# Zero-padded queries, reordered SSM output taps, an idle-tile first chunk and one merged gate/up stream in a decoder kernel

## The chip, the cores and the metric

The kernel runs on one core of a Trainium2 chip. The metric is the device time of one execution in microseconds (us). The engines are TensorE (PE in the profile, its weight loads apart as PEld), VectorE (DVE), ScalarE (ACT), GpSimd (POOL) and SyncE (SP), which here only issues DMAs.

## The reference

A batch of one, 256 positions, width 1024. Four decoder layers, each a mixer and a SwiGLU feed-forward block (FFN, hidden width 2816), and then a second block with attention and a state-space model (SSM) side by side:

```
for i in range(4):                                     # first_block
    hn = rms_norm(x, g[i, 0])
    m = (diff_attention, stick_breaking_attention, sliding_window_sink_attention)[i % 3](hn, ...)
    x = x + rms_norm(m, g[i, 1])
    h = rms_norm(x, g[i, 2])
    x = x + rms_norm((silu(h @ w_gate) * (h @ w_up)) @ w_down, g[i, 3])
# second_block
q, k, v, gate_a, u, gate_s = split(rms_norm_2(x, mix_norm) @ w_in)
attn = dilated_mixture_attention(q, k, v, ...) * silu(gate_a)       # 8 heads of 64
ssm  = s5_glu(u, ...) * silu(gate_s)                                # 32 groups of 16 channels, 64 complex states
x = x + concat(attn, ssm) @ w_out
x = x + sigmoid(rms_norm_2(x, ple_norm) @ w_ple_gate) * (p @ w_ple_proj)
```

Every head has 64 dimensions (the values of the differential attention 128). In the SSM the states follow x_t = a x_(t-1) + (B u)_t with complex a, and y = Re(C x) + D u, then a Gelu and a gated linear unit (GLU).

## The kernel before

The 256 positions are two row halves, b = 0 and 1, of 128 rows each. A weight matrix comes in chunks of 512 columns and all 1024 rows, in two DMAs of 1 MB into tiles `raw` (a ring of three). ScalarE rounds a weight to its upper part, DVE makes the lower part (`w<-raw`, a ring of 11 tiles `w`), and `gemm` multiplies in three passes: 24 matmuls `acc<-w,hnT` of 128 x 512 for each half and chunk. The chunks are steps: `run` lets half 1 follow half 0 by one step.

All instructions are first recorded by `_Program`. A list scheduler (`forward`, `backward`, `schedule`) then sets the order on every engine from modelled costs (`cost`, `passes`), and `issue` writes them out in that order. So every row of the trace has the line of `issue`: L478 before, L499 after, and rows are told apart by tile names and shapes.

The places around the change are these.

- **Scores.** Two heads of 64 dimensions lie one above the other in 128 rows of a tile `qk`. A score product takes the 64 rows of one head from q and k (`sc`, `z` and `sS` in the trace, with a weight tile of 64 rows). The attention of layers 0 and 3 is the differential one, of layer 1 the stick-breaking one, of layer 2 the one with sinks; `tr<-ident,rp` and `tr<-ident,qksb` are the transposes that make q and k. A layer's 16 heads come in two groups (`hg`), each with its own `qk` tile.
- **SSM preparation.** `ssm_prep_tasks` makes from the SSM's parameters the powers of a (`pp`, `q`), the tap products `ke` and the matrices E (input to chunk state) and G (state to output) for chunks of 8 positions. `part_e(q)` and `part_g(q)`, eight of each, are GpSimd operations of 256 columns (`pt`); `part_e` has four transposes `eT<-ident,pt` and four products `ke<-pt` on TensorE besides. The tasks run two a step from step 8 on, in the FFN of layer 0. Their results go to DRAM (`scrE`, `scrG`) and are loaded in the second block.
- **Output of the SSM.** `ssm_y` adds in PSUM `Y<-scrM,ssm` and the G products `Y<-scrG,ssm`: 128 products of 64 rows (one half of the states' rows, real or imaginary part), 32 columns of weights and 128 moving columns.
- **FFN.** The hidden width has 22 k-tiles of 128: two times eight, and a last part of six (four and two). Gate and up columns are chunks of their own, so the last two k-tiles are two chunks of 256 columns.
- **Start.** `setup` loads x transposed (`xT0`, four tiles), and the first weight chunk is loaded in pieces into `raw` tiles.
- **Pools.** `S8` is a ring of three big tiles of 2048 columns (`qk`, `v`, `facc`, `ssm`), `T8` one tile for each half.

Of the kernel before, what the change touches and what calls it, by code (L numbers as in the profile page):

```python
# [75 lines left out]
class _Chunk:  # L76
    def __init__(self, src, k0, nk, c0, n, cols=2048, head=False):
        self.src, self.k0, self.nk, self.c0, self.n = src, k0, nk, c0, n
# [12 lines left out]


class _Op:
    __slots__ = ("eng", "call", "args", "kw", "cost", "lat", "prio", "tiles", "pred", "succ", "n", "ready", "start",
                 "fin", "label", "step", "func", "cols", "idx", "passes", "group")
# [19 lines left out]
class _Program:  # L115
# [13 lines left out]
    TICK = 10240 / 3  # L129
    window = 6  # L130
# [54 lines left out]
    @staticmethod  # L185
    def dma_cost(out, src):
# [12 lines left out]
    def cost(eng, method, args, kw):  # L199
# [21 lines left out]
        return 150 + (2.1 if op == ALU.mult else 2.7) * n  # L221

    def record(self, eng, method, args, kw):
# [7 lines left out]
        if eng == "tensor":  # L231
            op.passes = self.passes(method, args)
            op.group = args[0].tensor.name
            op.cols = op.passes[1] * 2.4
# [73 lines left out]
    def forward(self, delta):  # L308
# [7 lines left out]
        order, table, group = [], None, None  # L316
# [3 lines left out]
        while len(order) < len(self.ops):  # L320
            for e in dirty:
# [17 lines left out]
                if e == "tensor" and best is not None and best.group != group:  # L339
                    for op in lst:  # L340
                        if op.group == group and op.ready <= f and op.prio <= best.prio + self.stick:
                            best = op
                            break
                if e == "tensor" and best is not None and best.cols < 100:
# [140 lines left out]
class _Net:  # L485
# [72 lines left out]
    def setup(self):  # L558
# [3 lines left out]
        xsrc = a["x"][0]  # L562
        self.gT = cp.tile([P, 80], F32, name="gT")
        nc.sync.dma_start(out=self.gT, in_=a["gT"])
        self.xT0 = []
        for b in range(NB):
            self.xT0.append([self.t2a(b, "xT0") for _ in range(2)])
        for h in range(2):
            nc.sync.dma_start(out=self.xT0[0][h], in_=a["xT"][:, h * 512:(h + 1) * 512])
# [3 lines left out]
        for h in range(2):  # L573
            nc.sync.dma_start(out=self.xT0[1][h], in_=a["xT"][:, 1024 + h * 512:1536 + h * 512])
        nc.sync.dma_start(out=self.x[0], in_=xsrc[:P, :])
        self.ident = cp.tile([P, P], F32, name="ident")
        nc.sync.dma_start(out=self.ident, in_=self.consts_dram[:, COFF["ident"][0]:COFF["ident"][0] + P])
        nc.sync.dma_start(out=self.x[1], in_=xsrc[P:, :])
        loads = [o for o in nc.ops if o.eng == "sync"]
        nc.head = [loads[i] for i in (3, 1, 0, 2, 4)] + loads[5:]  # L580
# [79 lines left out]
    def chunk(self, src, k0, nk, c0, n):  # L660
        c = _Chunk(src, k0, nk, c0, n, 2048 if self.chunks else 1024, not self.chunks)
# [4 lines left out]
    def prep(self, upto):  # L666
        nc = self.nc
        while self.prepped < min(upto, len(self.chunks)):
# [3 lines left out]
            for (k, m) in ch.units:  # L672
                sz = m * ch.n
                raw = self.nc.ring("raw", 3, self.rawp.tile([P, 2048], F32, tag="raw", name="raw"))
                src = ch.src[(ch.k0 + k) * P:(ch.k0 + k + m) * P, ch.c0:ch.c0 + ch.n]
                nc.sync.dma_start(out=raw[:, :sz].rearrange("p (k n) -> p k n", k=m),
                                  in_=src.rearrange("(k p) n -> p k n", p=P))
# [52 lines left out]
    def prenorm(self, b, g):  # L730
        nc, x = self.nc, self.x[b]
        xT = self.TA(b, "hnT")
        for h in range(2):
            k = slice(4 * h, 4 * h + 4)
            gk = self.gT[:, 8 * g + 4 * h:8 * g + 4 * h + 4]
            if g == 0:
                tp = gx = self.xT0[b][h].rearrange("p (j q) -> p j q", j=4)
            else:
                tp = self.xpose(b, x[:, h * 512:(h + 1) * 512], 4)
                gx = self.t2a(b, "gx").rearrange("p (j q) -> p j q", j=4)  # L740
# [49 lines left out]
    def mixer_steps(self, li, kind, inst):  # L790
# [24 lines left out]
        def qk_chunk(ch, hg, w, p0=0, first=False):  # L815
            def fn(b):
# [3 lines left out]
                if ("qk", hg) not in st:  # L820
                    st["qk", hg] = self.S8("qk").rearrange("p (w j t) -> p w j t", w=2, j=4)
                sc = 0.125 if w == 0 else 1.0
# [7 lines left out]
                nc.scalar.activation(st["qk", hg][:, w, p0:p0 + n, b * P:(b + 1) * P], tp[:, :n, :], AF.Copy, scale=sc)  # L830
# [899 lines left out]
```

## Time and profile before

| | before |
|---|---|
| median of 3 runs | 1418.18 us (1417.01 to 1419.39) |
| the profiled execution | 1417.66 us, its span 1415.5 us |
| TensorE busy | 1390.8 us, 98% |
| DVE / ScalarE / GpSimd busy | 899.2 / 771.7 / 168.1 us (64 / 55 / 12%) |
| DMA | 243.94 MB, 172 GB/s in the mean |

TensorE is busy nearly all the time. The page's chain that ended last is 87% TensorE, 5% GpSimd, 4% DVE. GpSimd's work lies mainly in four of the 40 slices of the span, those from 177 to 318 us. Times in rows count from the start of the span.

### The profile page before, as it was taken

The page shows a single profiled execution, that of the slowest core. Times are in us where ns is not written, and L with a number is a line of the kernel's source. Part 1 is how long each engine was busy: PE and PEld are TensorE (multiplying, and loading weights), DVE is VectorE, ACT ScalarE, POOL GpSimd, SP SyncE. Part 2 cuts the span into 40 slices and gives each one's busy share as a digit, 9 for nine tenths or more (in the row PEclk, how much of TensorE's full clock was granted, in tenths as well). Part 3 has the DMA queues.
Part 4 walks back from the last instruction along what each step waited for, and adds up shares of the span by engine and source line. Part 5 has one row for each costly group of instructions (what it writes and reads, how often), then busy time and mean ns, then how long its engine had stood idle before and what let it go on. Part 6 is the DMA issues. An engine that isn't in the chain of part 4 may idle for free.

```text
span 1415.5 us, 18447 instructions
## 1 busy us (share of the span) xinstructions
PE 1390.8 (98%) x7140; PEld 1145.2 (81%) x7140; DVE 899.2 (64%) x1307; ACT 771.7 (55%) x1258; POOL 168.1 (12%) x259
## 2 busy tenths in 40 slices
PE   7999998999999999999999999999999999999998
PEld 4788886878887888888888888888788888887786
DVE  6976664657655744557856545588766455677383
ACT  5666553435776645445755544465665444563572
POOL 0000069990000000000000000000010000020000
PEclk9999999999999999999999999999999999999999
DMA  7744564555532655563515555554446555565451
GB/s 258 232 139 131 194 223 163 186 174 194 201 118 91 204 198 178 178 200 131 190 60 193 165 194 200 172 181 154 144 164 201 186 178 163 166 235 187 150 174 42
DMA packets 130135, 243.94 MB, mean 172 GB/s; under 512 B 6032, under 2 KB 21392, under 8 KB 130048
## 3 DMA queue, kind: packets, MB, share of 16 engines
q1 hardware_dynamic: 130048, 242.77, 51.4%
q8 instruction: 56, 0.92, 0.3%
q14 instruction: 31, 0.25, 0.1%
HBM read 236.49 MB, written 6.26 MB: 171 GB/s over the span
## 4 chain that ended last, share of the span: by engine, by line
PE 87%; POOL 5%; DVE 4%; DMA 2%; ACT 1%; issue 1%; SPq 0%; DVEq 0%; ACTq 0%; POOLq 0%
PE acc L478 74%; PE tr L478 3%; POOL pt L478 3%; POOL pp L478 2%; PE sS L478 2%; PE sc L478 2%; PE z L478 1%; PE oS L478 1%; DVE w L478 1%; PE Y L478 1%; DMA raw<-in_w_ple_gate_dram 1%; PE o L478 1%; DVE scA L478 1%; PE asT L478 1%; POOL q L478 1%
## 5 line engine op out<-in xcount | busy, mean ns | idle before, releaser
L478 PE MATMUL acc<-w,hnT 128*128 128x512 f32 (+1 forms) x3744 | 846.4, 381 | 8.2 <-ACT hnT L478 3.1
L478 PEld LDWEIGHTS acc<-w,hnT 128*128 128x128 f32 x3744 | 665.8, 190 | 142.3 <-ACT hnT L478 5.5
L478 DVE TENSOR_TENSOR w<-raw,w 128x1024 fp32r<-128x1024 f32 (+1 forms) x431 | 518.6, 1218 | 203.5 <-ACT w L478 191.6
L478 ACT ACTIVATE w<-raw 128x1024 fp32r<-128x1024 f32 (+1 forms) x431 | 443.0, 1041 | 190.1 <-PE acc L478 156.6
L478 PE MATMUL acc<-w,hT 128*128 128x512 f32 x1056 | 251.7, 393 | 0.0
L478 PEld LDWEIGHTS acc<-w,hT 128*128 128x128 f32 x1056 | 196.5, 189 | 39.9
L478 PE MATMUL acc<-w,oT 128*128 128x512 f32 x480 | 120.6, 398 | 0.0
L478 POOL TENSOR_TENSOR po_r<-po_v,neghalf 128x1 f32<-128x1 f32 x16 | 12.7, 795 | 778.2 <-DVE po_v L478 778.2
L478 PEld LDWEIGHTS acc<-w,oT 128*128 128x128 f32 x480 | 87.3, 188 | 20.5 <-issue 3.3
L478 ACT ACTIVATE sg<-acc,pn_r 128x512 f32<-128x512 f32 (+1 forms) x48 | 31.2, 651 | 80.6 <-PE acc L478 80.5
L478 ACT ACTIVATE hT<-tr 128x512 fp32r<-128x512 f32 (+1 forms) x48 | 26.6, 556 | 72.6 <-PE tr L478 72.6
L478 DVE SCALAR_TENSOR_TENSOR sg<-acc,pn_r,sg 128x512 f32<-128x512 f32 (+1 forms) x48 | 33.8, 704 | 49.7 <-PE acc L478 45.0
L478 POOL TENSOR_TENSOR pt<-pp 128x256 f32<-128x256 f32 x64 | 55.4, 883 | 2.4 <-PE ke L478 1.6
L478 DVE TENSOR_TENSOR hT<-tr,hT 128x512 fp32r<-128x512 f32 (+1 forms) x48 | 30.8, 643 | 29.8 <-ACT hT L478 29.6
L478 DVE TENSOR_TENSOR facc<-acc,facc 128x512 f32<-128x512 f32 x32 | 21.9, 686 | 39.2 <-PE acc L478 39.2
L478 POOL TENSOR_TENSOR pn_r<-pn_v,neghalf 128x1 f32<-128x1 f32 x20 | 17.4, 871 | 211.3 <-DVE pn_v L478 205.5
L478 ACT ACTIVATE hnT<-gx 128x512 fp32r<-128x512 f32 x36 | 22.7, 629 | 22.9 <-DVE gx L478 22.8
L478 ACT ACTIVATE ad_e<-sc,ad_nm 128x128 f32<-128x128 f32 (+1 forms) x64 | 26.2, 422 | 15.2 <-DVE ad_nm L478 14.8
L478 POOL TENSOR_TENSOR pt<-pt 128x256 f32<-128x256 f32 x32 | 33.0, 1031 | 2.2
L478 ACT ACTIVATE sqj<-x 128x512 f32<-128x512 f32 x40 | 24.9, 625 | 10.7 <-DVE x L478 10.0
L478 DVE TENSOR_TENSOR hnT<-gx,hnT 128x512 fp32r<-128x512 f32 x36 | 24.7, 687 | 6.5 <-ACT hnT L478 5.8
L478 PE MATMUL tr<-ident,sg 128*128 128x128 f32 x176 | 27.3, 274 | 0.9 <-DVE sg L478 0.9
(221 smaller groups left out, 1077.7 us busy)
## 6 DMA issues: line engine op xcount, KB each, us to landing
raw<-in_ffn_w_gate_dram SPq DMA_DIRECT2D x44, 1024.0 KB, 5.2
raw<-in_ffn_w_up_dram SPq DMA_DIRECT2D x44, 1024.0 KB, 5.2
raw<-in_ffn_w_down_dram SPq DMA_DIRECT2D x32, 1024.0 KB, 5.2
raw<-in_a_w_in_dram SPq DMA_DIRECT2D x22, 1024.0 KB, 5.2
raw<-in_ffn_w_down_dram SPq DMA_DIRECT2D x16, 768.0 KB, 4.4
raw<-in_b_w_in_dram SPq DMA_DIRECT2D x12, 1024.0 KB, 5.4
raw<-in_w_in_dram SPq DMA_DIRECT2D x12, 1024.0 KB, 5.3
raw<-in_a_w_out_dram SPq DMA_DIRECT2D x8, 1024.0 KB, 5.1
```

The costliest lines, as they stand in the source:

```text
L478: r = getattr(getattr(self.nc, op.eng), op.call)(*op.args, **op.kw)
```

## The change

1. **Queries padded with zeros.** A q tile holds, for each half, two copies of 128 rows: in the first the rows of the lower head and zeros below, in the second zeros and the rows of the upper head. GpSimd writes the zeros (`zero_rows`), ScalarE one half of q and DVE the other. Scores multiply all 128 rows of k with one of the copies. In layers 0, 1 and 3 both head groups use the same q tile. The stick-breaking scores take two heads in one product.
2. **G by (real/imaginary, state) rows.** The matrix G lies in DRAM so that a product has the 128 rows of both parts of 64 states; 64 matmuls of 128 rows in place of 128 of 64 rows. The scanned states are copied into that layout (`scrX`, four copies on ScalarE and DVE).
3. **G a layer later.** C and the powers are saved to DRAM and loaded in the FFN of layer 1 (steps 34 to 42), where the `part_g` tasks run. Layer 0's FFN keeps one task a step.
4. **The first chunk** goes to tiles of the `S8` ring, which are idle at the start, and x transposed to a third; DMAs in another order, `prenorm` of the first layer by single chunks of 128 columns.
5. **The last gate and up columns** of each FFN are one chunk of 512.
6. **The scheduler** has a dearer GpSimd, a cost for changes of the array's shape (`mode`, `DRAIN`), and keeps products of one shape together.

The core of the diff:

```diff
+    def mode(method, args):
+        if method == "transpose":
+            return P, P
+        return tuple(P if n > 64 else 64 if n > 32 else 32 for n in (args[1].shape[0], _size(args[1])))
...
-        return 150 + (2.1 if op == ALU.mult else 2.7) * n
+        return 150 + (2.9 if op == ALU.mult else 3.5) * n
...
+                if op.mode != mode:
+                    if mode is not None:
+                        loader = max(loader, fin_pe + (self.DRAIN if op.mode == (P, P) else 0.0))
+                    mode = op.mode
...
+        if raws:
+            nc.head = [loads[1], raws[0], loads[0], raws[1], loads[2], raws[2], loads[3]] + raws[3:] + loads[4:]
...
+                if ch.idx:
+                    raw = self.nc.ring("raw", 3, self.rawp.tile([P, 2048], F32, tag="raw", name="raw"))
+                else:
+                    if k * ch.n % 2048 == 0:
+                        self.raw0 = self.S8("raw0")
...
+                if w == 0:
+                    q = self.q_tile(st, b, hg if kind == 2 else 0)
+                    nc.scalar.activation(q[:64, 0, p0:p0 + n, :], tp[:64, :n, :], AF.Copy, scale=0.125)
+                    nc.vector.tensor_scalar(q[64:, 1, p0:p0 + n, :], tp[64:, :n, :], 0.125, None, op0=ALU.mult)
...
+    def zero_rows(self, q):
+        self.nc.gpsimd.memset(q[64:, 0], 0.0)
+        self.nc.gpsimd.memset(q[:64, 1], 0.0)
...
-                    pr = slice(64 * c, 64 * c + 64)
-                    nc.tensor.matmul(banks[c][:, hh, :], qk[pr, 0, h, b * P:(b + 1) * P], qk[pr, 1, h, :nk * P],
+                    nc.tensor.matmul(banks[c][:, hh, :], q[:, c, h, :], k[:, h, :nk * P],
...
+                if m == 2:
+                    ch = self.chunk_of([(wg, c0, m * P), (wu, c0, m * P)], 0, KT)
+                    self.step(ch, gate_up(ch, part, kt))
...
+        early = [params, coef, powers] + [lambda q=q: part_e(q) for q in range(8)] + [save]
+        late = [load] + [lambda q=q: part_g(q) for q in range(8)]
...
+        X2 = self.scr_tile("scrX", 1024).rearrange("p (h g k) -> p h g k", h=2, g=16)
...
+                        nc.tensor.matmul(yp[h][32 * (2 * q + j):32 * (2 * q + j) + 32, g], X2[:, h, x, :],
+                                         G[:, j, g // 2, h, g % 2].rearrange("p (t f) -> p t f", t=8),
...
+            tasks = {8 + i: t for i, t in enumerate(early)} | {34 + i: t for i, t in enumerate(late)}
```

Three places of the order show what moved. On TensorE, in the FFN of layer 0, the first transposes and tap products of E (the first `eT` row of each list is part E1), before:

```order
L478 MATMUL eT<-ident,pt 128x128 x4
L478 MATMUL ke<-pt 128x32 x2
L478 MATMUL acc<-w,hnT 128x512 x19
L478 MATMUL ke<-pt 128x32 x2
L478 MATMUL acc<-w,hnT 128x512 x9
L478 MATMUL eT<-ident,pt 128x128
L478 MATMUL acc<-w,hnT 128x512 x11
L478 MATMUL eT<-ident,pt 128x128 x3
L478 MATMUL acc<-w,hnT 128x512 x9
L478 MATMUL ke<-pt 128x32 x4
```

and of the change:

```order
L499 MATMUL eT<-ident,pt 128x128 x4
L499 MATMUL ke<-pt 128x32 x4
L499 MATMUL acc<-w,hnT 128x512 x30
L499 MATMUL eT<-ident,pt 128x128 x3
L499 MATMUL ke<-pt 128x32 x3
L499 MATMUL acc<-w,hnT 128x512 x24
L499 MATMUL eT<-ident,pt 128x128
L499 MATMUL ke<-pt 128x32
L499 MATMUL acc<-w,hnT 128x512 x18
L499 MATMUL tr<-ident,sg 128x128 x4
L499 MATMUL eT<-ident,pt 128x128 x4
L499 MATMUL ke<-pt 128x32 x4
```

E2's first transposes stand 30 matmuls behind E1's in place of 28, and E3's 42 behind E2's last one. In all, 768 `acc` matmuls stand ahead of the first `eT` before, 744 in the change.

On GpSimd, the same place: the end of E1 and what follows it, before (`pt` of 128x256 are E, of 128x2x128 G; `pp` and `q` of 16 columns are powers):

```order
L478 TENSOR_TENSOR pt<-pp 128x256 x2
L478 TENSOR_TENSOR pp<-pp 128x16
L478 TENSOR_TENSOR pt<-pt 128x256
L478 TENSOR_TENSOR pt<-pp 128x2x128
L478 TENSOR_TENSOR pt<-pp 128x256
L478 TENSOR_TENSOR pp<-q_419 128x16
L478 TENSOR_TENSOR pt<-pt 128x2x128
L478 TENSOR_TENSOR q_419<-q_419 128x16
```

and of the change, from E1 on:

```order
L499 TENSOR_TENSOR pt<-pp 128x256 x3
L499 TENSOR_TENSOR pt<-pt 128x256
L499 TENSOR_TENSOR pp<-pp 128x16
L499 TENSOR_TENSOR pt<-pp 128x256
L499 TENSOR_TENSOR pp<-pp 128x16
L499 TENSOR_TENSOR pt<-pt 128x256
L499 TENSOR_TENSOR pp<-pp 128x16
L499 TENSOR_TENSOR pt<-pp 128x256
L499 TENSOR_TENSOR pp<-pp 128x16 x3
```

G's operations are gone from here. From E1's last `pt<-pt` to E2's last one the list of the change holds E2's six operations and 31 of 16 columns.

On TensorE, in the second block, the G products and what stands around them, before:

```order
L478 MATMUL Y_1939<-scrM,ssm 32x128 x8
L478 MATMUL Y_1939<-scrG,ssm 32x128
L478 MATMUL Y_1940<-scrM,ssm 32x128 x8
L478 MATMUL Y_1940<-scrG,ssm 32x128 x8
L478 MATMUL Y_1939<-scrG,ssm 32x128 x15
L478 MATMUL tr<-ident,qk2sb 128x128 x4
L478 MATMUL Y_1940<-scrG,ssm 32x128 x8
L478 MATMUL acc<-w,hnT 128x512 x9
L478 MATMUL Y_1939<-scrG,ssm 32x128 x8
L478 MATMUL Y_1940<-scrG,ssm 32x128 x16
L478 MATMUL Y_1939<-scrG,ssm 32x128 x8
```

and of the change:

```order
L499 MATMUL Y_1925<-scrM,ssm 32x128 x8
L499 MATMUL Y_1926<-scrM,ssm 32x128 x8
L499 MATMUL acc<-w,hnT 128x512 x31
L499 MATMUL Y_1925<-scrG,scrX 32x128 x8
L499 MATMUL Y_1926<-scrG,scrX 32x128 x8
L499 MATMUL acc<-w,hnT 128x512 x13
L499 MATMUL Y_1925<-scrG,scrX 32x128 x8
L499 MATMUL Y_1926<-scrG,scrX 32x128 x8
L499 MATMUL acc<-w,hnT 128x512 x5
L499 MATMUL yT<-ident,ssq 128x128 x8
```

The G products come in two groups of 16 entries (of two matmuls each in the trace). From the last of them to the end of the scores' fillers 45 `acc` matmuls stood before, and 21 stand now. Over the whole list TensorE changes between array shapes (128, 64 or 32 rows and columns of the weight tile) 129 times before and 37 times in the change.

## Rows read from the trace of the kernel before

**Rows 1.** The page, engines' busy time (us), share of the span, instructions.

```profile
PE 1390.8 (98%) x7140; PEld 1145.2 (81%) x7140; DVE 899.2 (64%) x1307; ACT 771.7 (55%) x1258; POOL 168.1 (12%) x259
```

**Rows 2.** Windows: length, PE, PEld, DVE, ACT, POOL busy, granted clock, DMA share, GB/s.

```profile
0.00:50.00 50.00, 40.81 (x162) 29.36 (x163) 37.50 (x81) 30.07 (x43) 1.32 (x6) 0.97 0.81 264
...
200.00:250.00 50.00, 44.44 (x204) 36.42 (x203) 25.61 (x30) 17.83 (x21) 48.36 (x112) 0.93 0.52 181
250.00:300.00 50.00, 46.52 (x215) 38.16 (x214) 28.02 (x32) 19.81 (x22) 48.09 (x55) 0.93 0.53 169
500.00:550.00 50.00, 50.00 (x228) 41.37 (x227) 25.26 (x23) 24.59 (x28) 0.00 (x0) 1.00 0.54 176
```

**Rows 3.** Timeline of TensorE at the start: start, length, idle time before and releaser.

```profile
26.10 0.73 PE L478 MATMUL acc<-w,hnT 128*128 128x512 f32 x2 [1.34 <-ACT w L478]
28.33 12.35 PE L478 MATMUL acc<-w,hnT 128*128 128x512 f32 x46 [1.50 <-DVE w L478]
```

**Rows 4.** Timeline of SP's queue at the start.

```profile
1.17 0.42 SPq L478 DMA_DIRECT2D xT<-in_xT_dram  x1
...
2.59 8.61 SPq L478 DMA_DIRECT2D raw<-in_a_w_in_dram  x4
```

**Rows 5.** A window of 2 us at the start, columns as in rows 2.

```profile
10.00:12.00 2.00, 1.90 (x5) 1.26 (x5) 1.51 (x4) 1.65 (x3) 0.00 (x0) 1.00 0.18 56
```

**Rows 6.** Waits of TensorE from 200 to 330 us: total, times, longest.

```profile
PE eT L478 <- POOL pt L478: 6.6, 3, 4.7
```

**Rows 7.** Groups of GpSimd's instructions: busy us, mean ns, idle before.

```profile
L478 POOL TENSOR_TENSOR pt<-pp 128x256 f32<-128x256 f32 x64 | 55.4, 883 | 2.4 <-PE ke L478 1.6
L478 POOL TENSOR_TENSOR pt<-pt 128x256 f32<-128x256 f32 x32 | 33.0, 1031 | 2.2
...
L478 POOL TENSOR_TENSOR pp<-q 128x16 f32<-128x16 f32 x14 | 3.1, 222 | 0.5
```

**Rows 8.** Timeline of TensorE, the transposes of E1 and E2.

```profile
226.92 0.60 PE L478 MATMUL eT<-ident,pt 128*128 128x128 f32 x4
...
239.52 0.47 PE L478 MATMUL eT<-ident,pt 128*128 128x128 f32 x1 [4.70 <-POOL pt L478]
```

**Rows 9.** Timeline of GpSimd, the last operation of E1.

```profile
218.26 0.74 POOL L478 TENSOR_TENSOR pt<-pt 128x256 f32<-128x256 f32 x1
```

**Rows 10.** Timeline of TensorE, scores and transposes in layer 0.

```profile
58.91 1.13 PE L478 MATMUL sc<-qk 64*128 64x256 f32 x4
...
68.03 1.13 PE L478 MATMUL sc<-qk 64*128 64x256 f32 x4
69.09 3.48 PE L478 MATMUL acc<-w,hnT 128*128 128x512 f32 x14
72.41 0.60 PE L478 MATMUL tr<-ident,rp 128*128 128x128 f32 x4
...
73.89 1.05 PE L478 MATMUL o<-v,ad_wT 128*128 128x128 f32 x8
74.70 0.47 PE L478 MATMUL acc<-w,hnT 128*128 128x512 f32 x1
```

**Rows 11.** Timeline of TensorE, end of the FFN of layer 0.

```profile
326.13 8.42 PE L478 MATMUL acc<-w,hT 128*128 128x512 f32 x36
334.39 4.48 PE L478 MATMUL acc<-w,hnT 128*128 128x256 f32 x36
338.71 0.60 PE L478 MATMUL eT<-ident,pt 128*128 128x128 f32 x4
```

**Rows 12.** Timeline of TensorE, the SSM's output in the second block.

```profile
1308.38 1.07 PE L478 MATMUL Y<-scrM,ssm 128*32 128x128 f32 x16
1309.37 0.40 PE L478 MATMUL Y<-scrG,ssm 64*32 64x128 f32 x2
...
1320.09 5.95 PE L478 MATMUL Y<-scrG,ssm 64*32 64x128 f32 x64
1325.97 3.75 PE L478 MATMUL acc<-w,hnT 128*128 128x512 f32 x15
```

More of the change, by code (lines that the diff above doesn't have):

```diff
@@ L76, with __init__ @@
 class _Chunk:
-    def __init__(self, src, k0, nk, c0, n, cols=2048, head=False):
-        self.src, self.k0, self.nk, self.c0, self.n = src, k0, nk, c0, n
+    def __init__(self, parts, k0, nk, cols=2048, head=False):
+        self.parts, self.k0, self.nk = parts, k0, nk
+        self.n = n = sum(m for _, _, m in parts)
         per = max(1, min(nk, cols // n))
@@ L315, in forward @@
                 ready[op.eng].append(op)
-        order, table, group = [], None, None
+        order, table, group, mode = [], None, None, None
         work = {}
@@ L343, in forward @@
                             break
+                if e == "tensor" and best is not None and best.mode != mode != (P, P):
+                    for op in lst:
+                        if op.mode == mode and op.ready <= f and op.prio <= best.prio + self.stick:
+                            best = op
+                            break
                 if e == "tensor" and best is not None and best.cols < 100:
@@ L561, in setup, with load @@
         self.x = [cp.tile([P, D], F32, name=f"x{b}") for b in range(NB)]
-        xsrc = a["x"][0]
         self.gT = cp.tile([P, 80], F32, name="gT")
[L564 to L569, printed above, removed]
+        loads = []
+        def load(out, src):
+            nc.sync.dma_start(out=out, in_=src)
+            loads.append(nc.ops[-1])
+        load(self.gT, a["gT"])
+        xs = self.S8("xT0").rearrange("p (k b q) -> p k b q", k=KT, b=NB)
+        self.xT0 = xs
+        for k, m in ((0, 2), (2, 2), (4, 4)):
+            load(xs[:, k:k + m].rearrange("p k b q -> p (k b q)"), a["xT"][:, k * 256:(k + m) * 256])
+        n = len(nc.ops)
         self.prepped = 0
@@ L673, in prep @@
                 sz = m * ch.n
[L674 to L677, printed above, removed]
+                if ch.idx:
[3 more added lines that the diff above has]
+                        self.raw0 = self.S8("raw0")
+                    o = k * ch.n % 2048
+                    raw = self.raw0[:, o:o + sz]
+                view = raw[:, :sz].rearrange("p (k n) -> p k n", k=m)
+                o = 0
+                for w, c0, n in ch.parts:
+                    src = w[(ch.k0 + k) * P:(ch.k0 + k + m) * P, c0:c0 + n]
+                    nc.sync.dma_start(out=view[:, :, o:o + n], in_=src.rearrange("(k p) n -> p k n", p=P))
+                    o += n
                 step = max(1, 1024 // ch.n)
@@ L1048, in stick_out @@
         per = 4 // nk
+        nj = 2 // nk
         oT = self.oT(st, b)
-        for u, aw in enumerate(aws):
+        for u in range(nk):
             op = self.sc("oB").rearrange("p (j q) -> p j q", j=4)
@@ L1348, in part_e, with save, load @@
                 nc.sync.dma_start(out=self.taps[112:, :], in_=st["ke"].rearrange("p g c -> p (g c)"))
+        def save():
+            nc.sync.dma_start(out=self.scr["P"][:, :512], in_=st["C"].rearrange("p r g c -> p (r g c)"))
+            nc.sync.dma_start(out=self.scr["P"][:, 512:], in_=st["PW"].rearrange("p k r g -> p (k r g)"))
+        def load():
+            t = self.S8("pg")
+            nc.sync.dma_start(out=t[:, :800], in_=self.scr["P"])
+            st["C"] = t[:, :512].rearrange("p (r g c) -> p r g c", r=2, g=16)
+            st["PW"] = t[:, 512:800].rearrange("p (k r g) -> p k r g", k=9, r=2)
+            st["gt"] = t[:, 800:928]
+            st["go"] = [t[:, 1024 + 512 * i:1536 + 512 * i] for i in range(2)]
@@ L1373, in scr_tile @@
+        return early, late
     def scr_tile(self, name, n):
```

256 lines of the change are left out of this document (143 added, 113 removed).

## The prediction

> **What bounds the kernel now.** I read the engines' busy time first: TensorE is busy for 1390.8 us of a span of 1415.5 us [rows 1]. So what counts is how long each product occupies TensorE, at which clock, and where it waits. Next come the windows: between 500 and 550 us TensorE is busy for the whole 50 us at a granted clock of 1.00, but in the first 50 us it is busy for 40.81 us, and in the two windows from 200 to 300 us for 44.44 and 46.52 us at a clock of 0.93 [rows 2]. Those are the stretches with something to win; the rest can only be won by giving TensorE less or cheaper work. The change touches both.
>
> **Start of the program.** TensorE pauses for 1.34 us ahead of 26.10 us and for 1.50 us ahead of 28.33 us, each time for one of the two halves into which ScalarE and DVE split a weight; from 28.33 us on 46 matmuls run in one row [rows 3]. Four weight loads hold SP's queue from 2.59 to 11.20 us [rows 4], since the raw ring has three buffers, and between 10 and 12 us only 56 GB/s move, against 264 in the mean of the first 50 us [rows 5, 2]. After the change nothing in the head waits for a raw buffer, so this dip should go: 2 us × (264 − 56)/264 = 1.6 us of transfer time. The clock of 0.97 in the first 50 us [rows 2] is a further 50 × 0.03 = 1.5 us, of which an unbroken stream would save part. I take −2.5. Bounds: 0 if DVE, not the loads, sets the resumption (the 28.33 us row waits for DVE), and −6 if the pauses of 26.10 and 28.33 us (1.34 + 1.50) go with both of the other items. The per-chunk prenorm costs ScalarE and DVE sixteen pieces each instead of four; they have 20 and 12.5 of these 50 us free [rows 2].
>
> **The SSM preparation (FFN of layer 0).** TensorE waits there 6.6 us in front of the E transposes for GpSimd's pt [rows 6]; the idle time of the two windows is 5.56 + 3.48 = 9.0 us, and the clock of 0.93 costs 2 × 50 × 0.07 = 7.0 us more [rows 2]. Together 16 us. GpSimd is busy for 48 us of each of these windows, so it is the bound: an E part and a G part are eight products at 0.883 and four sums at 1.031 us [rows 7], 11.2 us, as long as a step's 48 matmuls on TensorE, 48 × 0.229 = 11.0 us (the 0.229 is worked out below). Without G it needs 5.6 us a step. But the first parts still run against the powers: the order of after puts E2's transposes 30 matmuls (6.9 us) behind E1's, and GpSimd's list between E1's last sum and E2's last one has E2's six operations (5.6 us) and 31 of 16 columns, which at 0.22 us are 6.8 us [rows 7]. In before E1 was finished at 219.00 us and its transposes ran at 226.92 us, 7.9 us of slack [rows 8, 9]; 24 fewer matmuls (5.5 us) stand ahead of them now, so 2.4 us of it are left. E2 then waits for 5.6 + 6.8 less 6.9, 2.4 and about 1 of transposes and tap products: 2.1 us; before it waited 4.7 us [rows 8]. I leave 3 us of waiting and half of one of the two windows' slow-clock cost of 3.5 us (1.75). 16 − 4.75 makes −11. Bounds: −16 if nothing waits, −4 if E2's wait keeps its 4.7 us and the clock falls twice as before. G's 96 operations now run in the next layer's FFN, where no product of TensorE follows from them and GpSimd has no other long work; their 32 stores and one load are issued by SP at 0.42 us each [rows 4], 14 us of a queue that is ahead of TensorE there, and I cost them at nothing.
>
> **Scores in full height, and fewer changes of array shape.** Four score products of 64 rows and 256 columns take 69.09 − 68.03 = 1.06 us, while eight full-height products of 128 columns, the same number of columns, take 74.70 − 73.89 = 0.81 us [rows 10]. A visit to the half-height shape thus costs 0.25 us beside its columns. By the order lists TensorE changes shape 129 times before and 37 times after; the 92 changes saved are 46 visits, 46 × 0.25 = 11.5. Some of them are those of the G products, counted below, and the stick-breaking scores now run two heads in one product, so I take −10. Bounds −8 (the G visits out) and −15 (46 × 0.33, if waiting for loads is saved too). The price of the zeros is GpSimd's memsets: it is busy for 1.32 of the first 50 us [rows 2], and otherwise idle outside layers 0 and 1; the other halves of q go to DVE, one operation for each.
>
> The Trainium skill, "TensorEngine Tiling (Array Packing)", section "Theoretical Speedup", speaks against this edit: products with a contraction of at most 64 can run in two row tiles at up to twice the speed, which zero-padding to 128 rows gives up. By it the padded four would take 2.12 us. The trace does not agree: two tiles side by side would make the four products of 64 rows cheaper than the full-height ones, and they are dearer.
>
> **Gate and up of the last six k-tiles.** 36 products of 256 columns take 338.71 − 334.39 = 4.32 us, 0.120 each; 36 of 512 take 334.39 − 326.13 = 8.26 us, 0.229 each [rows 11]. 384 narrow ones become 192 wide ones: 192 × (0.240 − 0.229) = −2. The four loads of 512 KB for two of 1 MB move the same bytes.
>
> **The G products of the last block.** 64 products in 5.88 us are 0.092 us each, against 16 of scrM in 0.99 us, 0.062 each [rows 12]. Before: 128 × 0.092 = 11.8 us. After: 64 at 0.062 to 0.092, 4.0 to 5.9 us. That is 5.9 to 7.8 us less work. But there is little to put in its place: behind the last Y product 45 acc matmuls filled the way to the scores before, and now 21 stand there, with ScalarE's copies of Y in between [rows 12]; and four copies for the new X tile are on the scan's chain. I take −5, bounds 0 and −8. I add +1 for small new waits.
>
> **Sum.** Against the profiled execution's own 1417.66 us (span 1415.5 us; the runs shown have a median of 1418.18 us, 0.5 more): −2.5 − 11 − 10 − 2 − 5 + 1 = −29.5, so **1388 us**.
>
> **Rivals.**
> *GpSimd still sets the pace of layer 0's FFN* (0.13). For: the chain of E parts and powers above is longer than the stream that covers it. Against: from E3 on there are about 5.6 us of work a step. Only 4 of the 11 are won: 1395; with the start at 0 it is 1398.
> *The last block keeps its time* (0.10): the path is then scan, Y, Gelu, GLU, and TensorE waits for ScalarE. For: the fillers are down from 45 to 21. 1388 + 5 = 1393.
> *More is won than the terms say* (0.08): start −6, preparation −16, shapes −15; 1388 − 3.5 − 5 − 5 = 1374 or below.
> *The shared q tile makes TensorE wait, slower than before* (0.04). In layers 0, 1 and 3 both head groups use one q tile, so group 1's q of a half can only be written when group 0's scores of that half are done. Before, group 1's transposes ran at 72.41 us, 3.3 us behind the end of the other group's last scores at 69.09 us [rows 10], so this margin is thin. Score units of one half lie up to 68.03 − 58.91 = 9.1 us apart. There are six such places; the wait decides from (1418 − 1388)/6 = 5 us each, and at 7 us each it is 1388 + 42 = 1430. Against: 14 acc matmuls stand between in the same rows, and the static order can put the second q behind more of them.
> *Half-height products overlap, and padding gives that up* (0.02): each four products then take twice 1.06 us; some 44 visits × 1.06 = +47 in place of the −10: 1388 + 10 + 47 = 1445. The rows of 1.06 against 0.81 us speak against it. (It is the rule of the Trainium skill, "TensorEngine Tiling (Array Packing)", cited above.)
> *The start wins nothing, or the shapes only 8* is inside the range of the main case.
>
> **How the numbers follow.** The forecast itself has 0.63. Its own range, with two of its terms short or long at a time (start 0 and preparation −5: 1396.5; shapes −15 and preparation −16: 1378), is 1378 to 1397. The first two rivals lie inside or at its upper edge, so 1373 to 1400 holds 0.83 of the chance. A measurement of this kernel tells about 0.2% (2.8 us) from no change. Faster by more than that: main, the first three rivals, 0.94; slower: the lost overlap 0.02 and half of the shared q tile's 0.04; within 0.2%: the other half, with waits of about 5 us each, 0.02.
>
> **What would show it.** Right: no row of TensorE with a 64-row tile; the windows between 200 and 300 us with TensorE idle for some 3 us and a clock near 1.00 in the second; no 256-column acc products; 64 G products at 0.062 to 0.092 us; the stream resumes at about 25 to 26 us. Wrong: waits for pt at every E part; a wait of TensorE for asT, yT or the Gelu's output in the last 90 us; the wait of a q transpose or of a score product for a q written late; a clock below 1.00 in a new place.

## The result and the profile after

The changed kernel takes 1393.21 us (median of 4 runs, 1392.37 to 1393.89) against 1418.39 us of the kernel before on the same chips: a ratio of 0.9823 (95% interval 0.9806 to 0.984), 25.2 us less. Forecast were 1388 us, in a range of 1373 to 1400. The profiled execution took 1392.37 us, its span is 1390.5 us.

The page's busy time, answering to [rows 1]:

```profile
PE 1365.8 (98%) x6836; PEld 1126.5 (81%) x6836; DVE 910.1 (65%) x1337; ACT 768.3 (55%) x1270; POOL 197.3 (14%) x331
```

TensorE is busy for 25.0 us less, as much as the span is shorter, and still bounds the kernel. Its idle time, the span less its busy time, is 24.7 us in both kernels. The windows of [rows 2]:

```profile
0.00:50.00 50.00, 41.65 (x171) 30.97 (x172) 40.70 (x96) 33.99 (x69) 3.38 (x10) 0.93 0.76 261
...
200.00:250.00 50.00, 45.80 (x216) 38.03 (x215) 25.12 (x34) 20.82 (x24) 41.13 (x90) 0.93 0.44 146
250.00:300.00 50.00, 50.00 (x243) 41.95 (x242) 28.96 (x33) 18.84 (x22) 17.15 (x19) 1.00 0.58 189
500.00:550.00 50.00, 50.00 (x226) 41.39 (x225) 25.80 (x22) 24.49 (x28) 45.04 (x71) 1.00 0.65 206
```

The second window of the preparation is full and at full clock, the first is not. GpSimd's G is now in the window from 500 us, where TensorE stays busy for 50.00 us. But the first 50 us are no better than before: 0.84 us more of work, and a clock of 0.93 in place of 0.97.

To see where the time went I cut both traces at the same amount of work: a stage ends with the start of a given `acc` product, counted in trace order (512 columns count one, 256 a half; the two traces count 5064 each). The numbers are 384, 1176, 1560, 2352, 2568, 3360, 3744 and 4536, which is 48 for every chunk of 512 columns and 1024 rows; other products lie between in either order, so an edge is good to about 1 us. "First" is the start of the first product, and the second block ends with the start of the last one. Times in us:

| kernel | first | L0 mixer | L0 FFN | L1 mixer | L1 FFN | L2 mixer | L2 FFN | L3 mixer | L3 FFN | second block |
|---|---|---|---|---|---|---|---|---|---|---|
| before | 7.1 | 127.2 | 213.9 | 123.3 | 187.9 | 89.6 | 187.4 | 114.4 | 187.7 | 172.0 |
| after | 8.0 | 122.8 | 203.2 | 120.5 | 187.3 | 88.0 | 187.5 | 116.0 | 187.3 | 165.0 |
| difference | +0.9 | −4.4 | −10.7 | −2.8 | −0.6 | −1.6 | +0.1 | +1.6 | −0.4 | −7.0 |

The two places named in the prediction carry most of it: layer 0's FFN and the second block. Layer 3's mixer became slower.

### The profile page after: what moved, and what is told of

It reads as the page before. It is cut to its first block, busy times and chain, and to the rows that moved or that the text cites. A ratio compares the mean times of both kernels' runs of the same rounds, so it can differ in the third digit from the quotient of the medians.

```text
span 1390.5 us, 18011 instructions
## 1 busy us (share of the span) xinstructions
PE 1365.8 (98%) x6836; PEld 1126.5 (81%) x6836; DVE 910.1 (65%) x1337; ACT 768.3 (55%) x1270; POOL 197.3 (14%) x331
## 4 chain that ended last, share of the span: by engine, by line
PE 82%; DVE 9%; POOL 3%; ACT 3%; issue 1%; DMA 1%; SPq 0%; DVEq 0%; ACTq 0%; POOLq 0%
PE acc L499 71%; DVE w L499 3%; PE tr L499 3%; POOL pp L499 2%; DVE rp L499 1%; PE z L499 1%; PE sc L499 1%; PE sS L499 1%; PE oS L499 1%; ACT w L499 1%; PE o L499 1%; POOL pt L499 1%; ACT sqj L499 1%; PE asT L499 1%; DVE x L499 0%
## 5 line engine op out<-in xcount | busy, mean ns | idle before, releaser
L499 PEld LDWEIGHTS acc<-w,hnT 128*128 128x128 f32 x3552 | 654.3, 189 | 141.1 <-ACT w L499 6.2
L499 POOL TENSOR_TENSOR pg<-pg 128x128 f32<-128x128 f32 x96 | 61.8, 668 | 38.9 <-PE acc L499 35.9
L499 ACT ACTIVATE sqj<-x 128x512 f32<-128x512 f32 x40 | 25.0, 625 | 10.5 <-DVE x L499 10.4
L499 POOL TENSOR_TENSOR ad_r<-ad_v,neghalf 128x4 f32<-128x4 f32 x8 | 8.1, 1012 | 147.0 <-DVE ad_v L499 139.0
L499 PEld LDWEIGHTS tr<-ident,sg 128*128 128x128 f32 x176 | 21.9, 141 | 8.0 <-DVE sg L499 2.4
```

The lines of the kernel that those rows point to most:

```text
L499: r = getattr(getattr(self.nc, op.eng), op.call)(*op.args, **op.kw)
```

## The experiments

All are compared by their medians with the kernel before, timed beside them in three groups (medians 1418.92, 1419.56 and 1418.87 us), and their stages, each from one profiled execution, with those of the changed kernel's trace. Intervals are of the ratio to the kernel before.

**Half-height scores** (half_rows). Scores of the differential, sink and dilated attention over 64 rows again, everything else as in the change:

```diff
-                    nc.tensor.matmul(banks[c][:, hh, :], q[:, c, h, :], k[:, h, :nk * P],
+                    pr = slice(64 * c, 64 * c + 64)
+                    nc.tensor.matmul(banks[c][:, hh, :], q[pr, c, h, :], k[pr, h, :nk * P],
```

> The changed kernel with the score products of the differential, sink and dilated attention taken over 64 rows again, from the same zero-padded q tiles and in the changed scheduler (the stick-breaking scores stay at 128 rows). My theory, each visit to the half-height shape costs 0.2 to 0.3 us beside its columns: the score rows sum up to some 6 to 7 us more and the kernel takes +5 to +8 us (1398 to 1401). Rival, that half-height products overlap and the padding gave that up: the kernel becomes faster, by up to 15 us. Rival, that the scheduler hides the shape changes: within 2 us of the changed kernel.

1405.11 us, ratio 0.9907 (0.9891 to 0.9923): 12 us more than the change. Its stages: L0 mixer +1.3, L1 mixer 0.0 (its scores were left at 128 rows), L2 mixer +3.2, L3 mixer +2.5, second block +4.1. They sum up to some 11 us, more than the 5 to 8 I expected, but a stage moves with the order alone too, the second block by 10 us (the seeds below). The score rows by themselves, summed from start to start without idle time, take 49.2 us against 41.9 in the change: 7.3 us, close to the 6 to 7 expected.

The same sixteen sink scores of 128 columns in layer 2, first in half_rows, then in the changed kernel (timelines of TensorE: start, length, shape, count):

```profile
654.42 2.28 PE L499 MATMUL sS<-kvC,q 64*128 64x128 f32 x16
656.63 1.82 PE L499 MATMUL acc<-w,hnT 128*128 128x256 f32 x13
```

```profile
653.32 2.02 PE L499 MATMUL sS<-kvC,q 128*128 128x128 f32 x16
655.10 1.07 PE L499 MATMUL acc<-w,hnT 128*128 128x256 f32 x7
```

From start to start that is 2.21 us against 1.78, with zeros in half of the rows: 0.43 us for this visit, when the columns are the same. And four products of 256 columns in the changed kernel:

```profile
54.29 1.10 PE L499 MATMUL sc<-k,q 128*128 128x256 f32 x4
55.04 1.97 PE L499 MATMUL acc<-w,hnT 128*128 128x512 f32 x7
```

0.75 us, where before took 1.06 us [rows 10].

These visits don't test whether products of the two row halves run side by side. Each half writes a PSUM tile of its own, and the signal to that tile's reader comes with its last product. In the visit at 654.42 us the signals come with the 8th and the 16th product, and a visit of four has one signal, with the 4th: the order puts all products of one half in front of those of the other. Where it takes the halves in turn, they do overlap. Eight products of 256 columns in half_rows, one half behind the other (signals with the 4th and the 8th) and then in turn (with the 7th and the 8th), and in the change:

```profile
61.42 1.88 PE L499 MATMUL sc<-k,q 64*128 64x256 f32 x8
63.23 4.38 PE L499 MATMUL acc<-w,hnT 128*128 128x512 f32 x18
...
957.34 1.14 PE L499 MATMUL sc<-k,q 64*128 64x256 f32 x8
958.41 5.96 PE L499 MATMUL acc<-w,hnT 128*128 128x512 f32 x25
```

```profile
952.36 1.97 PE L499 MATMUL sc<-k,q 128*128 128x256 f32 x8
953.97 4.71 PE L499 MATMUL acc<-w,hnT 128*128 128x512 f32 x19
```

That is 1.81 us, 1.07 us and 1.61 us. In the visit of 1.07 us the products start in pairs, 13 or 14 ns apart. So the rival beside which the prediction cited the Trainium skill, "TensorEngine Tiling (Array Packing)", section "Theoretical Speedup", is not refuted: this visit agrees with a speedup of up to 2×, with 1.81 to 1.07 us. What half_rows shows is that zeros beat the order that the scheduler gives to half-height products, mostly one half behind the other. Half height with the halves kept in turn was not run.

**G back in layer 0** (early_g). The tasks E and G in turn, two a step, G's layout and products as in the change:

```diff
-        early = [params, coef, powers] + [lambda q=q: part_e(q) for q in range(8)] + [save]
-        late = [load] + [lambda q=q: part_g(q) for q in range(8)]
-        return early, late
+        tasks = [params, coef, powers, tiles]
+        for q in range(8):
+            tasks.append(lambda q=q: part_e(q))
+            tasks.append(lambda q=q: part_g(q))
+        return tasks, []
```

> The changed kernel with G's parts back in the FFN of layer 0, E and G in turn, two tasks a step as before; layout and products as in the change. My theory, G's 45 us of GpSimd there make TensorE wait and let its clock fall: waits for pt of 8 to 12 us and a clock of 0.93 in both windows between 200 and 300 us, the kernel +8 to +12 us (1401 to 1405). Rival, that the scheduler's dearer GpSimd places the transposes late enough: at most +3 us.

1422.05 us, ratio 1.0023 (1.0009 to 1.0037): the whole gain of the change is gone, and more. The waits stand elsewhere than I said: layer 0's FFN is 4.6 us shorter than in the change and layer 1's mixer 22.2 us longer; the second block, where no G is made, is 10.4 us longer. The order has the last E parts behind the FFN, and there they are waited for (waits of TensorE from 200 to 370 us, total, times, longest; then its timeline):

```profile
PE eT L499 <- POOL pt L499: 15.7, 4, 5.8
```

```profile
339.94 0.69 PE L499 MATMUL eT<-ident,pt 128*128 128x128 f32 x2 [5.78 <-POOL pt L499]
...
357.36 0.47 PE L499 MATMUL eT<-ident,pt 128*128 128x128 f32 x1 [4.01 <-POOL pt L499]
360.96 0.90 PE L499 MATMUL eT<-ident,pt 128*128 128x128 f32 x3 [2.85 <-POOL pt L499]
```

GpSimd had time for them. One small operation of the norm behind the FFN stands in its list ahead of the remaining parts, and GpSimd is idle for 63.86 us in front of it (timeline of GpSimd):

```profile
320.69 0.55 POOL L499 TENSOR_TENSOR po_r<-po_v,neghalf 128x1 f32<-128x1 f32 x1 [63.86 <-DVE po_v L499]
```

So this run shows a bad order, not that GpSimd is too slow for E and G in layer 0, and it doesn't price the move of G.

**G later alone** (before_late_g). The kernel before with `save`, `load`, and G's tasks in layer 1's FFN, one task a step and G's operations in pieces of 128 columns as in the change, and nothing else of it:

```diff
+        early = [params, coef, powers] + [lambda q=q: part_e(q) for q in range(8)] + [save]
+        late = [load] + [lambda q=q: part_g(q) for q in range(8)]
...
+            tasks = {8 + i: t for i, t in enumerate(early)} | {35 + i: t for i, t in enumerate(late)}
```

> The kernel before with one part of the change alone: G's tasks, with C and the powers saved and loaded again, in the FFN of layer 1, E's tasks one a step in layer 0; scheduler, scores, G's layout and products as before. My theory, the preparation term of the prediction: the stretch from the 488th to the 1064th full-width acc product (159.9 us in the kernel before, 149.8 in the changed one) falls by 8 to 13 us, and so does the time (1405 to 1411). Rival, that E2's wait for the powers and the clock's fall behind it stay whole: -3 to 0 us in that stretch.

1417.93 us, ratio 0.9997 (0.9986 to 1.0008): no gain that can be measured. The stretch that I named fell by 8.8 us (159.9 to 151.1), as forecast, and layer 0's FFN by 9.8. But layer 1's FFN rose by 8.7. (Layer 0's mixer, in which nothing was changed, fell by 6.5 us, to 120.7: a first sign of what the order does.) The cause of the 8.7 is in the queue of SP (timeline of SP, then the ScalarE and TensorE rows):

```profile
559.86 0.34 SPq L478 DMA_DIRECT2D scrG<-pg  x1
560.29 0.39 SPq L478 DMA_DIRECT2D raw<-in_ffn_w_down_dram  x1
566.98 0.34 SPq L478 DMA_DIRECT2D scrG<-pg  x1
567.41 0.39 SPq L478 DMA_DIRECT2D raw<-in_ffn_w_down_dram  x1
```

```profile
573.60 1.06 ACT L478 ACTIVATE w<-raw 128x1024 fp32r<-128x1024 f32 x1 [5.67 <-DMA raw<-in_ffn_w_down_dram]
```

```profile
575.20 5.23 PE L478 MATMUL acc<-w,hT 128*128 128x512 f32 x12 [6.46 <-ACT hT L478]
580.26 5.60 PE L478 MATMUL acc<-w,hnT 128*128 128x512 f32 x24
```

A store of G waits at the head of the queue until GpSimd has made G, at 566.98 us. The last load of down weights stands behind it, is issued at 567.41 us, and ScalarE waits for it until 573.60 us; the operation on hT stands behind that weight on ScalarE, and TensorE idles for 6.46 us. The twelve products behind the pause take 580.26 − 575.20 = 5.06 us, 0.42 each in place of 0.229, at a granted clock of 0.58 from 575 to 581 us: 2.3 us more, and with the pause 8.8. The timeline's releaser names hT; the cause is three queues further back. SP waited for GpSimd's pg in front of eight stores:

```profile
SPq L478 <- POOL pg L478: 46.2, 8, 8.4
```

**The old GpSimd cost** (old_pool_cost). The changed kernel with the scheduler's old figure for GpSimd:

```diff
-        return 150 + (2.9 if op == ALU.mult else 3.5) * n
+        return 150 + (2.1 if op == ALU.mult else 2.7) * n
```

> The changed kernel with the old, too cheap GpSimd costs in the scheduler (256 columns at 688 and 841 ns by its model where the trace has 883 and 1031). My theory, with G out of layer 0 GpSimd needs 5.6 us a step, so the cost matters only for E2: waits for pt of 4 to 8 us, +0 to +5 us. Rival, that the dearer cost was what took away the waits: pt waits of 8 us or more and the slow clock in both windows, +8 us or more.

1405.90 us, ratio 0.99 (0.9885 to 0.9915): 12.7 us more than the change, 6.2 of it in layer 0's FFN, 3.4 in layer 1's, 9.0 in the second block, less 2.6 in layer 0's mixer. Waits for pt and for the tap products from 200 to 370 us, and the window from 200 us:

```profile
PE eT L499 <- POOL pt L499: 5.2, 3, 4.8
PE ke L499 <- DVE pt L499: 1.9, 1, 1.9
```

```profile
200.00:250.00 50.00, 43.13 (x197) 35.13 (x196) 24.69 (x34) 18.29 (x23) 38.30 (x90) 0.90 0.45 142
```

The 9.0 us of the second block, where GpSimd hardly works, are no effect of its cost that I can name; other orders below have 169.5 to 175.5 us there, so the draw of the order is enough for them. For the two FFNs the result lies between my theory and its rival.

**The powers of a^8 later** (q8_late), and the same with two other seeds of the scheduler (q8_seed: 347, q8_seed2: 348; the change has 346):

```diff
-        early = [params, coef, powers] + [lambda q=q: part_e(q) for q in range(8)] + [save]
+        early = [params, coef, powers] + [lambda q=q: part_e(q) for q in range(8)] + [powers8, save]
```

> The changed kernel with the powers of a^8 (42 short GpSimd operations) taken out of the powers task and put behind the last E part. My theory, these are what E2 and E3 wait for: the 4.2 us of waits for pt and the clock's fall behind them go, -5 to -8 us (1385 to 1388). Rival, that E1 to E2 stays as long because the scheduler packs E's six operations tighter against TensorE: -2 to 0 us.

> The powers of a^8 behind the last E part, with the scheduler's seed 347. Theory: no wait for pt in the preparation whatever the draw (141 to 144 us for its stretch), the rest by the draw: 1382 to 1394. Rival, that the powers were not the cause and seed 346 only drew a better order: waits for pt of 3 us or more.

> The same with seed 348. Theory: no wait for pt (141 to 144 us for the preparation's stretch), 1382 to 1394. Rival: waits for pt of 3 us or more in this draw.

q8_late: 1387.19 us, ratio 0.978 (0.9765 to 0.9794), 6 us less than the change, and its wait for pt is gone. That looked like my theory. The other two seeds took 1400.79 us (0.987, 0.985 to 0.9889) and 1409.19 us (0.9929, 0.9912 to 0.9945), and they wait. TensorE's waits for pt in q8_late from 200 to 370 us, in q8_seed and in q8_seed2:

```profile
PE eT L499 <- POOL pt L499: 0.3, 1, 0.3
```

```profile
PE eT L499 <- POOL pt L499: 5.4, 3, 2.7
```

```profile
PE eT L499 <- POOL pt L499: 6.8, 2, 5.3
```

With seed 346 the edit wins 6.0 us, with seed 347 it loses 4.9 (seed below, 1395.91, against 1400.79). So the theory falls: the powers alone are not the cause, and q8_late is a good order, not a good edit. As a kernel it is the fastest of this study.

**Another seed, alone** (seed: the change with 347; before_seed: the kernel before with 347):

```diff
-    tries, seed = 24, 346
+    tries, seed = 24, 347
```

> The changed kernel with the scheduler's random seed 347 in place of 346 and nothing else: the work is the same, only the order differs. My theory, after the first four runs: the order alone moves the time by some 5 us, with gains and losses in the start, in the preparation and in the last block, so one kernel's end time can't price an edit of less than that: between 1386 and 1400. Rival, that the order is nearly settled and the other runs' stage times differ for their edits: within 1.5 us of 1393.

> The kernel before with the scheduler's random seed 347 and nothing else. Theory: the order moves its time as it moved the stages of the changed kernel, by up to 8 us in the start, the preparation or the last block, and by less than 2 us in the stretch from the 1640th to the 4520th acc product; so 1411 to 1426. Rival, that the order of before was a good draw among worse: 1425 or above.

seed: 1395.91 us, ratio 0.9828 (0.9812 to 0.9845); before_seed: 1422.30 us, ratio 1.002 (1.0009 to 1.0032). The sums agree within 3 to 4 us, the stages don't. In seed TensorE's wait for pt is 0.6 us although the powers are in their old place, layer 0's FFN is 4.5 us shorter than in the change and the second block 7.2 us longer. Stages of six kernels that do the change's work in different orders (those named q8 with the powers later, q8_head with another start too), beside the two orders of before:

| kernel | L0 mixer | L0 FFN | L1 mixer | L3 mixer | second block | median |
|---|---|---|---|---|---|---|
| before | 127.2 | 213.9 | 123.3 | 114.4 | 172.0 | 1418.4 |
| before_seed | 125.9 | 215.0 | 125.3 | 114.2 | 174.4 | 1422.3 |
| after | 122.8 | 203.2 | 120.5 | 116.0 | 165.0 | 1393.2 |
| seed | 121.5 | 198.7 | 119.8 | 115.7 | 172.2 | 1395.9 |
| q8_late | 123.1 | 196.5 | 119.7 | 116.5 | 169.5 | 1387.2 |
| q8_seed | 121.6 | 206.2 | 119.8 | 117.1 | 175.5 | 1400.8 |
| q8_seed2 | 123.2 | 204.6 | 125.6 | 116.5 | 175.1 | 1409.2 |
| q8_head | 121.8 | 204.0 | 119.2 | 116.2 | 171.1 | 1400.1 |

Gains that hold in all six orders: 3 to 6 us in layer 0's mixer and 8 to 19 us in its FFN. A loss of 1 to 3 us in layer 3's mixer holds in all six too. But six orders of one side are not enough for the mixers: before_late_g, with the start, the scores and the scheduler of before, has 120.7 us in layer 0's mixer and 116.1 in layer 3's. Of layer 0's mixer the score rows are 1.9 to 2.5 us in every order (12.0 us before, 9.5 to 10.0 in the six); that the rest comes from the change is not shown. The second block ranges over 10 us, and the change's own order has the best of it.

**The start** (old_head: the start of before in the changed kernel, with the raw ring, four tiles of x and the old order of loads; q8_head: q8_late with the gains and the second chunk's first half further ahead in SP's queue):

```diff
-                if ch.idx:
+                if True:
...
-            nc.head = [loads[1], raws[0], loads[0], raws[1], loads[2], raws[2], loads[3]] + raws[3:] + loads[4:]
+        nc.head = [loads[i] for i in (3, 1, 0, 2, 4)] + loads[5:]
```

```diff
-            self.prep(1)
+            self.prep(2)
...
-            nc.head = [loads[1], raws[0], loads[0], raws[1], loads[2], raws[2], loads[3]] + raws[3:] + loads[4:]
+            nc.head = [loads[1], loads[0], raws[0], raws[1], loads[2], raws[2], loads[3]] + raws[3:6] + loads[4:] + raws[6:]
```

> The changed kernel with the start of before: first chunk through the raw ring, x transposed in four tiles, old order of the loads, norm in halves. My theory, the new head is worth 2 to 4 us at the 73rd matmul and 2.5 at the end of the first input projection: +2 to +4 us (1395 to 1397). Rival, that DVE's work behind the first chunks sets the pace of the start and the head is worth nothing: within 1 us.

> The powers of a^8 behind the last E part, and at the start the gains and the second chunk's first half ahead of x on SP's queue (its second half right behind x and the identity, ahead of the small constants). Theory: the start of the change gave its lead back because ScalarE's first operation waited for the gains (first product at 7.95 us) and the second chunk came behind x and three small loads, which let the clock fall; so the first product comes at about 6.5 us, the stream stands no longer than 1 us at 22 to 25 us and the time is 1380 to 1385. Rival, that DVE is the limit behind 24 us anyway: same as with the powers alone, 1387.

old_head: 1394.15 us, ratio 0.9829 (0.9815 to 0.9844), within 1 us of the change. Its first product comes 2.0 us later and its 49th product 5.0 us later, but its 200th product starts at 72.7 us against 73.0 in the change (75.5 in before). q8_head: 1400.14 us, ratio 0.9862 (0.9845 to 0.9878); first product at 7.8 us, not 6.5, the 200th at 71.4 us, and a wait for pt of 4.2 us in layer 0's FFN. Both fit the rival that something behind the first chunk sets the pace, but they don't show it: the order alone puts the 200th product at 69.7 (seed) to 75.3 us (q8_seed2), and at 70.7 us in before_late_g, which has the start of before. That DVE, which the next section shows busy, is the limit was not tried by itself.

**Narrow gate and up** (narrow_gate): the last two k-tiles as two chunks again.

```diff
-                if m == 2:
+                if m == 0:
```

> The changed kernel with the last two k-tiles' gate and up columns as two chunks of 256 again (384 narrow products). My theory: by the rows of before 2 x 0.120 against 0.229 us, some 2 us more on TensorE, of which a new draw of the order can hide or add up to 5 us; 256-column rows sum up to about 46 us. Rival, that merging also takes away waits at the end of each FFN: +4 us or more, with TensorE idle ahead of rows of the last part.

1399.03 us, ratio 0.9855 (0.984 to 0.9869): 5.8 us more. The FFNs of layers 1 to 3 take 1.3, 0.6 and 1.1 us more, 1.0 each in the mean, which is hardly more than orders differ there (187.1 to 189.5 us in layer 1's FFN over the six). The acc products on hnT, summed from start to start without idle time, take 820.5 us against 817.7 in the change: 2.8 us, near my theory's 2. Layer 0's FFN is 3.3 us shorter and the second block 7.7 us longer, in which there is no such chunk: the draw again.

## Why the prediction held, step by step

The sum was 29.5 us, measured are 25.2. The range and the direction held, and the number in part by luck: of the six orders above three took more than 1400 us, the upper end of the range. The preparation, the rows of G and those of gate and up are right for their reason; the scores' sum is right with a reason that holds only in part; the start's term is not shown to be there at all; and the new waits were taken far too small.

**Start, −2.5: not shown.** At its 200th product the changed kernel is 2.5 us ahead, but so is old_head (2.8), and the order alone moves that point by more. The timeline of TensorE, answering to [rows 3]:

```profile
7.95 0.49 PE L499 MATMUL acc<-w,hnT 128*128 128x512 f32 x1 [3.38 <-ACT w L499]
8.68 13.03 PE L499 MATMUL acc<-w,hnT 128*128 128x512 f32 x47 [0.23 <-DVE w L499]
22.27 0.73 PE L499 MATMUL acc<-w,hnT 128*128 128x512 f32 x2 [0.56 <-ACT w L499]
24.86 7.12 PE L499 MATMUL acc<-w,hnT 128*128 128x512 f32 x23 [1.86 <-DVE w L499]
31.82 0.60 PE L499 MATMUL tr<-ident,rp 128*128 128x128 f32 x4
```

The stream resumes at 24.86 us, as the prediction's mark said (25 to 26). Then 23 products take 31.82 − 24.86 = 6.96 us, 0.30 each in place of 0.229: the clock has fallen (0.83 in the mean of the window from 24 to 34 us, in both kernels). So the clock's part of the term went the other way: 0.93 in place of 0.97 in the first 50 us, 2 us more, where part of 1.5 was to be saved. And the next limit is there, in a window of 10 us and a row of TensorE's timeline:

```profile
24.00:34.00 10.00, 9.14 (x35) 7.41 (x36) 10.00 (x17) 4.70 (x7) 0.00 (x0) 0.83 0.81 267
```

```profile
46.38 0.63 PE L499 MATMUL tr<-ident,rp 128*128 128x128 f32 x4 [1.23 <-DVE rp L499]
```

DVE is busy for all 10.00 us (9.65 in before) and TensorE later waits 1.23 us for its rope. That is the bound of 0 that I gave for the head, and these rows fit it.

**Preparation, −11: confirmed, −10.7.** In layer 0's FFN TensorE's idle time fell from 9.0 to 4.2 us, and one of the two slow-clock windows went, worth 3.5 us; G moved alone wins 9.8 us there (before_late_g). The wait left at E2 was worked out as 2.1 us and taken as 3; it is 4.2 in two pieces, at E2 as said, and one of the two slow-clock windows stayed, of which I had taken half:

```profile
217.11 7.07 PE L499 MATMUL acc<-w,hnT 128*128 128x512 f32 x30
227.23 0.47 PE L499 MATMUL eT<-ident,pt 128*128 128x128 f32 x1 [3.04 <-POOL pt L499]
228.87 0.69 PE L499 MATMUL eT<-ident,pt 128*128 128x128 f32 x2 [1.17 <-POOL pt L499]
```

The slack of 2.4 us was there: E1's last sum ends at 213.31 us and its transposes start at 215.86. Short was the price of the 31 operations of 16 columns, 0.22 us each or 6.8 in all: they took 10.7 us, four of them 1.1 to 1.3 us each, and I can't say why (timeline of GpSimd, the first of the four):

```profile
215.22 1.27 POOL L499 TENSOR_TENSOR pp<-q 128x16 f32<-128x16 f32 x1
```

What failed in this step is the sentence that G's stores cost nothing, "a queue that is ahead of TensorE there". before_late_g shows a price of 8.7 us in layer 1's FFN, as much as the move wins. The change doesn't pay it: layer 1's FFN takes 187.3 us, and ScalarE waits there for down weights for 0.4 us, against 11.4 in before_late_g. With the old cost alone put back these waits are 10.9 us, TensorE waits 3.0 us for sg, and the stage takes 190.7 us. So the price seems to depend on where the planner's cost of GpSimd puts the stores; with one order each it is not shown that the cost decides it (q8_late, with the new cost, has 9.1 us of these waits, and TensorE loses 0.8).

**Scores, −10: the sum right, the reason only in part.** The score rows, summed from start to start without idle time, fell from 52.2 to 41.9 us, by 10.3, and they take 42.1 and 43.0 us in the orders seed and q8_late. Four products of one half fell from 1.06 us to 0.67 to 0.88; in the second block:

```profile
1312.06 1.03 PE L499 MATMUL sS<-k,ssq 128*128 128x256 f32 x4
1312.93 0.27 PE L499 MATMUL sS<-m_causal,identb 128*128 128x256 bf16 x1
```

What failed is the price of 0.25 us for every visit, and the sentence that the trace doesn't agree with products side by side: the four products of 1.06 us are all of one half and can't show it. By stage the rows fell by 2.5 us in layer 0, 3.7 in layer 1 (where one product also takes two heads now), 3.1 in layer 2, 0.8 in the second block, and by 0.2 in layer 3. There two visits of before had the halves partly in turn and took 1.27 and 1.38 us, less than the 1.61 of the padded products, so there was nothing to win:

```profile
968.85 1.34 PE L478 MATMUL sc<-qk 64*128 64x256 f32 x8
970.12 5.97 PE L478 MATMUL acc<-w,hnT 128*128 128x512 f32 x25
```

The 1.6 us that layer 3's mixer lost are idle time for 1.0 us (1.36 against 0.37 in before), in two waits for DVE, which writes half of q now:

```profile
932.89 0.63 PE L499 MATMUL tr<-ident,rp 128*128 128x128 f32 x4 [0.98 <-DVE rp L499]
988.23 0.76 PE L499 MATMUL adT<-ident,ad_e 128*128 128x128 f32 x4 [0.23 <-DVE ad_e L499]
```

Whether that is DVE's half of q, the q tile shared by the head groups (the rival on the other side, in a mild form) or the draw was not told apart.

**Gate and up, −2:** −2.8 by narrow_gate's rows. In the change against before the FFNs of layers 1 to 3 differ by −0.6, +0.1 and −0.4 us, where three quarters of it should be seen; in part that is new idle time, 1.1 us in these three.

**G's products, −5: the rows better than forecast, the sum a draw.**

```profile
1302.08 1.94 PE L499 MATMUL Y<-scrG,scrX 128*32 128x128 f32 x32
1303.95 3.24 PE L499 MATMUL acc<-w,hnT 128*128 128x512 f32 x13
```

32 records in 1.87 us are 0.058 each, below the lower end of 0.062: 64 × 0.058 = 3.7 us for 11.8. The second block won 7.0 us. But the other five orders have 169.5 to 175.5 us there, and before has 172.0 and 174.4: in the mean of six, 171.4, next to nothing is left. The rows are not what gives way: all products on Y, those of scrM with them, take 7.5 us in each of the six, against 16.5 and 15.4 in the two orders of before. TensorE idles more in this stage, 2.9 to 6.5 us in the six against 1.4 and 2.3. The discount for the thin filler was right in kind and too small; what takes back the rest was not followed.

**New waits, +1:** the largest mis-sized term. TensorE's idle time is 24.7 us before and after, although 4.8 us of it went from layer 0's FFN; so 4.8 us came elsewhere, 2.2 of them in the second block. All of the 25 us won is busy time: the scores' rows 10.3, G's 8, gate and up nearly 3, and the clock some 1.5 (3.5 won in the preparation, 2 lost at the start); some 2 us of the 25 I can't place.

Of the rivals, GpSimd's pace and the last block's time were both within the range; the last block's is what the mean of the six orders shows. That half-height products overlap is so where the halves come in turn, and in those visits of before padding gave something up; the +47 us of that rival supposed it in every visit. A q wait that makes the kernel slower didn't come.

## What to carry to other kernels

When a scheduler draws the order, the time of one build is a draw too: here nearly the same work took 1387 to 1409 us in six orders, and a stage 10 us more or less. Cut the traces at equal work and run a second seed before an edit of less than 1% is believed or dropped. And when work is moved to an idle engine, look at who carries its results away: a store that waits at the head of an in-order queue holds every load behind it, so plan the stores with the move. And before a price is put on a shape, see which products of it the order puts side by side: the same eight took 1.81 or 1.07 us.

## What the runs showed of the hardware

Sixteen score products of 128 columns over 64 rows, one row half behind the other, took 2.21 us and over 128 rows, half of them zeros, 1.78 us: against that order zero-padding cost TensorE nothing. Eight products of 256 columns over 64 rows took 1.81 us one half behind the other and 1.07 us with the halves in turn, against 1.61 us padded: products of the two row halves run side by side when they come in turn. Products with 32 columns of weights ran at 0.058 us over 128 rows against 0.092 over 64 [rows 12], so twice the rows cost less time, not the same.
